# A hybrid decoder step on one core: the constants' place in VectorE's queue, and the PSUM banks of the output units

## The chip, the cores and the metric

The kernel runs on one core of one Trainium2 chip. The metric is the device time of one execution in microseconds (us), as the median of several runs. The engines are named as in the profile: PE is TensorE's matmuls and PEld its weight loads, DVE is VectorE, ACT is ScalarE, POOL is GpSimd, SP is SyncE, which here issues the DMAs (SPq).

## What is computed

The reference is one step of a decoder with two layers, for a prompt of 2048 tokens and a batch of 8 × 4 sample tokens, at a width of 1024. Cut to what matters:

```
def even_mixer(h, w_in, ...):                       # layer 0
    proj = h @ w_in
    qa, fa, ia, ga, qb, kb, vb, gb, fb = _split(proj, ...)
    f = lb + (1.0 - lb) * sigmoid(fa)
    o_a, s_a = gated_linear_chunked(qa, 1.0 - f, ia, log(f), hgrn_s0)
    o_a = head_rmsnorm(o_a, hgrn_gain) * silu(ga)
    o_b = fox_attend(qb, kb, vb, log_sigmoid(fb + b_fox)) * silu(gb)
    out = concatenate([o_a, o_b]) @ w_out
...
def odd_mixer(h, w_in, w_gate, ...):                # layer 1
    q, k, v, g, r = _split(h @ w_in, ...)
    log_f = log_sigmoid(r @ w_gate + b_gate) / 16
    o, s = gated_linear_chunked(q * scale, k, v, log_f, gla_s0)
    o = head_rmsnorm(o, gla_gain) * silu(g)
    return o @ w_out, s
...
x = x + even_mixer(rmsnorm(x, norm_even), ...)      # run_trunk
x = x + odd_mixer(rmsnorm(x, norm_odd), ...)
return rmsnorm(x, final_norm), ...                  # and the caches and states
```

`lb` is a softmax over the two rows of `lb_logits`; `fox_attend` is causal attention with forget gates, and for the sample tokens over paged caches.

## The kernel before, in words

Each large product is cut into **units**: 256 columns of a weight matrix by one half of the tokens (1024 prompt tokens, and in the half 0 the 32 sample rows as well). The operands are kept in two parts of 16 bits, so each product of a 128-row block is three matmuls (`mm3`, L595 to L597), and eight such blocks make a sum. A unit has four steps: `fetch` loads its raw weights (`wr_...`, L330), `measure` and `scale` find a power of two that fits them (VectorE's `rm_...` and `pow_...`, L264 to L305), and `split` makes the two parts (`w_...`: ScalarE L348, L354, L355, VectorE L349, POOL L356). They are run some units ahead (`staged`). `proj_fm` computes a unit with features on the partitions, in column pieces (`pf_...`); `proj_tm` computes one with tokens on the partitions, in pairs of 128-token tiles (`pt_...`), and `few_rows` adds the sample rows (`pS_...`).

The phase of layer 0 begins with the norm of the first half, in groups: ScalarE squares a row block (L429), VectorE makes the scale (L406, POOL L408) and scales the rows (`nx_...`, L431), TensorE transposes them (`nt_...`, L455), and ScalarE and VectorE in turn write the result in two parts (`act`, L590 and L591). The first unit, v0 (`pt_Av`), is multiplied beside these groups. The second unit, g0 (`pf_Ag`), makes the gate: `silu2` copies a piece (ScalarE L651), takes the tanh (`th_A`, L652) and multiplies it in (`sg`, VectorE L653). The third, qf0 (`pf_A00f`, weights `w_Aqf`), is the first to need `fa`, `fb` and `fbn`.

These, and other constants that no unit needs before, are made by `more_consts`: the gains `g_hgrn` and `g_gla` (L168), the chain of `lb` (L175 to L189, with two exponentials on ScalarE, L178 and L179), the gate's weights `wg` (a memset of `wgr` L194, three loads L196, ScalarE's copy L198, VectorE L199), seven masks `mlev` (POOL L206 to L210 into `mtmp`, a cast on VectorE L213), `mdiag` (L216) and zeros in two tiles `scT` (L235).

The order of each engine's queue is not the order of the code: the framework has a scheduler that runs a timeline of its own and puts every instruction where its operands allow it. `tc.issue_after(x)` holds it back: within it, the instructions of the engine that x runs on are put behind x; those of other engines aren't held. `more_consts` is called under three such holds: behind `last_x` (a load on SP), `last_a` and `last_th` (both on ScalarE). So VectorE's and POOL's constants are held by nothing but their operands.

Behind layer 0's attention stage the output projections run, four **out units** for each half and layer (`out_units`). In the trace the half 1 of layer 0 runs from about 1380 to 1481 us, and it is followed by the first units of layer 1 (`pt_Cv`, ...). While an out unit's tiles (`pt_o`) are multiplied, VectorE adds each to a block of x that has been loaded (`xo`, L1825), and the result is stored (L1827); beside it, the rows of x are normed for layer 1 (`x1r`, L533 to L547) and stored as `xs`, and DMA transposes bring them back as `act` (L565, on SP). An out unit has its own weights (`w_o`), prepared as above. `done` marks the last stage, in which the final norm is run beside it.

PSUM has eight banks, in four groups by tag: `pj` 3, `gr` 2, `st` 1 and `o` 2. All units' tiles come from `pj`; `gr` and `o` are those of the norm's transposes at the start, and later of the linear attention.

Of the kernel before, what the change touches and what calls it, by code (L numbers as in the profile page):

```python
# [8 lines left out]
F32 = mybir.dt.float32  # L9
# [6 lines left out]
ALU = mybir.AluOpType  # L16
# [3 lines left out]
P = 128  # L20
# [89 lines left out]
def drain(g):  # L110
    for _ in g:
        pass
# [11 lines left out]
class Kern:  # L124
    def __init__(self, ctx, tc, ins, outs):
        self.ctx, self.tc, self.nc = ctx, tc, tc.nc
        self.i, self.o = ins, outs
        self.loaded = {}


    def consts(self):
# [473 lines left out]
            evac(ps[:M, :n], c0, n)  # L605
            yield 24 * (n / 2.4 + 3)

    def proj_tm(self, pps, act, W, hf, evac, nm, width=256, pairs=True):

        tl = self.ttiles(hf)  # L610
        per = 2 if width == 256 and pairs else 1
        for g in range(0, len(tl), per):
            grp = tl[g : g + per]
            n = grp[0][1]
            if n < P:
                evac(self.few_rows(pps, act, W, grp[0][0], nm, width), g, 1, n)
                yield 700
                continue
            ps = pps.tile([P, per, width], F32, tag="pj", name=f"pt_{nm}{g}")
            for j, (c0, n) in enumerate(grp):  # L620
                for k in range(KT):
                    self.mm3(ps[:n, j], [x[:, k, c0 : c0 + n] for x in act],
                             [x[:, k, :width] for x in W], k == 0, k == KT - 1)
            evac(ps[:n, : len(grp)], g, len(grp), n)
            yield 24 * len(grp) * 110
# [21 lines left out]
    def silu2(self, wp, dst, ps, n, nm, c):  # L647

        nc = self.nc
        th = wp.tile([P, 512], F32, tag="th", name=f"th_{nm}")  # L650
        nc.scalar.activation(dst, ps, AF.Copy, scale=c)  # L651
        self.last_th = nc.scalar.activation(th[:, :n], dst, AF.Tanh, scale=0.5)  # L652
        nc.vector.scalar_tensor_tensor(dst, th[:, :n], 1.0, dst, ALU.add, ALU.mult)  # L653


    def lin_attn(self, wp, pps, hf, h, dv, q, f, k, v, vs, sg, gain, S, s0, s_out, p_out, ydst, nm):
# [418 lines left out]
    def phase_even(self):  # L1075
        tc, nc, i = self.tc, self.nc, self.i
# [3 lines left out]
        with pool("act", side="right") as ap, pool("w", side="right") as w0, pool("wl", side="right") as wp1, \  # L1080
# [4 lines left out]
            pps = Pool(pp0, {"pj": 3, "gr": 2, "st": 1, "o": 2})  # L1085
# [6 lines left out]
            act = self.alloc_act(ap)  # L1092
# [19 lines left out]
            for hf in range(2):  # L1112
# [7 lines left out]
                def dense(a, b, hf=hf):  # L1120
                    return self.staged(us, 16 * hf + a, 16 * hf + b, beside)

                lin = lins[hf]
                if hf == 0:
                    groups = self.norm_groups(nrm, pps, act, hf, get_x, self.g_even)
                    groups[0][0]()
                    for step in us[0][0]:
                        self.ready[0] = step()

                    for g in groups[1:3]:  # L1130
                        g[2]()

                    def behind(ins, g):
                        with tc.issue_after(ins.ins):
                            groups[g][0]()

                    def turn0():
                        groups[0][1](1, lambda st: st.enter_context(tc.issue_after(self.last_scale.ins)))

                    def turn1():  # L1140
                        groups[1][1](KT // 2 - 1, lambda st: behind(self.last_a, 2))
                        behind(self.last_a, 3)

                    steps = [lambda: None, lambda: behind(self.last_split, 1), lambda: None, lambda: None, groups[4][0]]
                    turns = [turn0, turn1] + [g[1] for g in groups[2:]]
                    first = self.handover(list(zip(steps, turns)), dense(0, 1), last)
                    drain(first)
                    second = dense(1, 2)
                    for _ in range(2):
                        next(second)  # L1150
                    with tc.issue_after(self.last_x.ins), tc.issue_after(self.last_a.ins), \
                            tc.issue_after(self.last_th.ins):
                        self.more_consts(wp)
                    drain(second)
                else:
                    self.sx_odd = self.gain_scale(self.g_odd, pps, "pj", "o")
                    self.later = [self.later_unit(wpool, pps, w, cols, key, undo) for w, cols, key, undo in
                                  self.later_units()]
                    first = dense(0, 1)
                    for g in nxt:  # L1160
                        c = next(last, None)
                        g[1]()
                    drain(last)
                    drain(first)
# [640 lines left out]
    def out_units(self, hf, layer, act, wpool, wp, pps, x2=None, done=None):  # L1805

        nc, i = self.nc, self.i
        w = i[("w_out_even", "w_out_odd")[layer]][0]

        def mk(u):  # L1810
            cs = slice(u * 256, (u + 1) * 256)
            undo = [self.kcol()] + ([self.kcol()] if layer == 0 and hf == 0 else [])

            def ev(ps, g, cnt, m):
                c0 = self.ttiles(hf)[g][0]
                c = undo[-1 if m < P else 0][:m]
                if x2 is None:
                    if layer:
                        t = wp.tile([P, 2, 256], F32, tag="c2", name=f"xo{layer}{hf}{u}{g}")
                    else:  # L1820
                        t = wp.tile([P, HALF + TS], F32, tag="c4", name=f"xo{layer}{hf}{u}{g}")[:, :512].rearrange(
                            "p (g d) -> p g d", g=2)
                    src = self.rows(hf, c0, m * cnt, layer == 0)[:, cs].rearrange("(g p) d -> p g d", g=cnt)
                    nc.sync.dma_start(t[:m, :cnt], src)
                    nc.vector.scalar_tensor_tensor(t[:m, :cnt], ps, c, t[:m, :cnt], ALU.mult, ALU.add)  # L1825
                    dst = self.rows(hf, c0, m * cnt, False)[:, cs].rearrange("(g p) d -> p g d", g=cnt)
                    nc.sync.dma_start(dst, t[:m, :cnt])  # L1827
                else:
                    for j in range(cnt):
                        d = x2[g + j][:m, cs]  # L1830
                        nc.vector.scalar_tensor_tensor(d, ps[:, j], c, d, ALU.mult, ALU.add)
                        if done:
                            done(u, g + j, x2[g + j], cs)
                        if layer == 0 and u == 3:
                            nc.sync.dma_start(self.rows(hf, c0 + j * P, m, False), x2[g + j][:m])

            return (self.half_unit(wpool, pps, w, [(u * 256, 256)], f"o{layer}{u}", f"o{layer}{hf}{u}",
                                   also=list(zip(undo, (self.sy[layer], self.sy[2]))),
                                   raw=("yr", 256) if (hf, layer, u) == (0, 0, 0) else ("wr", WU),
                                   scaler="pool" if (hf, layer, u) == (0, 0, 0) else None),  # L1840
                    lambda W: self.proj_tm(pps, act, W, hf, ev, f"o{layer}{hf}{u}", pairs=not done or u < 3))

        return [mk(u) for u in range(4)]


# [343 lines left out]
```

## Time and profile before

| | before |
|---|---|
| runs | 2366.59, 2371.02, 2367.46 us, median 2367.46 |
| profiled execution | 2365.9 us, its span 2364.2 |
| PE busy | 2265.2 us, 96% of the span |
| DVE, ACT, POOL busy | 59%, 46%, 35% |
| granted TensorE clock, mean | 0.989 |

The span goes from the first to the last instruction of the profiled execution; its own time includes what lies around it. Rows of the waits view give the engine, its tile and line, then whom it waited for: us in total, how often, the longest. Rows of the timeline give the start and the duration in us, the engine, the line, the operation and its tiles, and in brackets how long the engine had been idle before and what ended it. Rows of the windows view give a stretch, its length, busy us and count of instructions for PE, PEld, DVE, ACT and POOL, then the granted clock (1.00 is full), the DMA engines' share, and GB/s.

### The profile page before, as it was taken

The page shows a single profiled execution, that of the slowest core. Times are in us where ns is not written, and L with a number is a line of the kernel's source. Part 1 is how long each engine was busy: PE and PEld are TensorE (multiplying, and loading weights), DVE is VectorE, ACT ScalarE, POOL GpSimd, SP SyncE. Part 2 cuts the span into 40 slices and gives each one's busy share as a digit, 9 for nine tenths or more (in the row PEclk, how much of TensorE's full clock was granted, in tenths as well). Part 3 has the DMA queues.
Part 4 walks back from the last instruction along what each step waited for, and adds up shares of the span by engine and source line. Part 5 has one row for each costly group of instructions (what it writes and reads, how often), then busy time and mean ns, then how long its engine had stood idle before and what let it go on. Part 6 is the DMA issues. An engine that isn't in the chain of part 4 may idle for free. (4 is left out here: it accounts for less than half of the span.)

```text
span 2364.2 us, 58202 instructions
## 1 busy us (share of the span) xinstructions
PE 2265.2 (96%) x23124; PEld 1613.1 (68%) x23124; DVE 1404.4 (59%) x3225; ACT 1090.3 (46%) x2372; POOL 818.6 (35%) x858
## 2 busy tenths in 40 slices
PE   6999999999999999999999999999899999999998
PEld 5667667864655875655445888777677666666887
DVE  6656557536664538666767444366675655557554
ACT  5434343333333226556667543436545545545333
POOL 3133324112212226234557345144452422222223
PEclk9999999999999999999999999999999999999999
DMA  6231334755441267776873867633234431115453
GB/s 191 73 89 59 100 109 146 196 157 148 145 123 56 75 196 239 239 256 198 280 239 117 278 197 249 148 96 108 79 117 101 107 103 57 48 55 166 152 194 149
DMA packets 358004, 344.89 MB, mean 146 GB/s; under 512 B 90994, under 2 KB 300723, under 8 KB 357731
## 3 DMA queue, kind: packets, MB, share of 16 engines
q1 hardware_dynamic: 356226, 336.64, 46.8%
q8 instruction: 182, 2.98, 0.5%
q0 software_dynamic: 1504, 4.52, 0.5%
q14 instruction: 92, 0.75, 0.1%
HBM read 248.73 MB, written 79.63 MB: 139 GB/s over the span
## 5 line engine op out<-in xcount | busy, mean ns | idle before, releaser
L595 PE MATMUL pt_o<-w_o,act 128*128 128x256 f16 x1024 | 281.1, 274 | 8.2 <-DVE xo L1825 6.6
L597 PE MATMUL pt_o<-w_o,act 128*128 128x256 f16 x1024 | 281.0, 274 | 3.8 <-DVE act L1784 3.7
L596 PE MATMUL pt_o<-w_o,act 128*128 128x256 f16 x1024 | 281.1, 275 | 1.5 <-POOL w_o L356 1.5
L597 PEld LDWEIGHTS <-act 128*128 128x128 f16 x2304 | 227.3, 99 | 39.4 <-DVE act L1784 5.1
L596 PEld LDWEIGHTS <-act 128*128 128x128 f16 x2304 | 227.3, 99 | 38.5 <-issue 8.4
L595 PEld LDWEIGHTS <-act 128*128 128x128 f16 x2304 | 227.4, 99 | 35.9 <-issue 3.4
L761 POOL TENSOR_TENSOR kA<-kA,fA 128x512 f32<-128x512 f32 (+1 forms) x56 | 79.5, 1419 | 190.1 <-PE gl_A L727 141.9
L595 PE MATMUL pt_Cv<-w_Cv,act 128*128 128x256 f16 (+1 forms) x512 | 141.4, 276 | 0.0
L597 PE MATMUL pt_Cv<-w_Cv,act 128*128 128x256 f16 (+1 forms) x512 | 141.3, 276 | 0.0
L596 PE MATMUL pt_Cv<-w_Cv,act 128*128 128x256 f16 (+1 forms) x512 | 141.3, 276 | 0.0
L761 POOL TENSOR_TENSOR kC<-kC,fC 128x512 f32<-128x512 f32 (+1 forms) x56 | 83.6, 1493 | 153.8 <-PE gl_C L727 102.5
L1392 ACT ACTIVATE L<-L,nm,kc 128x512 f32<-128x512 f32 (+3 forms) x160 | 118.2, 741 | 33.5 <-DVE nm L1390 27.8
L1400 POOL TENSOR_SCALAR L<-L,nm 128x512 f32<-128x512 f32 (+3 forms) x160 | 99.0, 632 | 64.5 <-DVE nm L1396 23.9
L1427 ACT ACTIVATE th<-pt 128x512 f16<-128x512 f32 (+3 forms) x159 | 80.5, 528 | 64.5 <-PE pt L1420 63.6
L1428 DVE TENSOR_TENSOR tl<-pt,th 128x512 f16<-128x512 f32 (+3 forms) x159 | 94.6, 609 | 21.4 <-ACT th L1427 20.5
L1420 PE MATMUL pt<-ident,L 128*128 128x128 f32 x544 | 91.2, 279 | 7.1 <-POOL L L1400 4.2
L1420 PEld LDWEIGHTS pt<-ident,L 128*128 128x128 f32 x544 | 66.6, 143 | 33.3 <-DVE tl L1428 8.3
L1544 PEld LDWEIGHTS pkt<-ident,pgcache_fox_k 128*128 128x128 f32 x512 | 57.4, 141 | 42.7 <-issue 25.1
L1877 ACT ACTIVATE vC<-pt_Cv,kc 128x512 f32<-128x512 f32 (+1 forms) x40 | 23.9, 598 | 129.9 <-PE pt_Cv L597 129.9
L1544 PE MATMUL pkt<-ident,pgcache_fox_k 128*128 128x128 f32 x512 | 75.1, 278 | 7.3 <-DVE kts L1548 5.1
L1825 DVE SCALAR_TENSOR_TENSOR xo<-pt_o,kc,xo 128x512 f32<-128x512 f32 x48 | 35.8, 748 | 62.0 <-PE pt_o L597 57.2
L597 PE MATMUL pt_Av<-w_Ai,act 128*128 128x256 f16 x256 | 70.9, 277 | 1.5 <-DVE act L591 1.5
(957 smaller groups left out, 6788.5 us busy)
## 6 DMA issues: line engine op xcount, KB each, us to landing
pgcache_fox_k<-in_cache_fox_k SPq DMA_DIRECT2D x128, 256.0 KB, 4.4
pgcache_fox_v<-in_cache_fox_v SPq DMA_DIRECT2D x128, 256.0 KB, 4.3
yr<-yT SPq DMA_DIRECT2D x16, 1024.0 KB, 7.2
x1d<-xo SPq DMA_DIRECT2D x48, 256.0 KB, 4.1
wr_Aqf<-in_w_in_even SPq DMA_DIRECT2D x64, 128.0 KB, 3.2
wr_o<-in_w_out_even SPq DMA_DIRECT2D x32, 256.0 KB, 6.0
xo<-in_x_prompt SPq DMA_DIRECT2D x32, 256.0 KB, 4.2
wr_Cv<-in_w_in_odd SPq DMA_DIRECT2D x32, 256.0 KB, 3.8
```

The source lines that it names most:

```text
L595: nc.tensor.matmul(ps, lh[0], rh[0], start=first, stop=False)
L596: nc.tensor.matmul(ps, lh[0], rh[1], start=False, stop=False)
L597: return nc.tensor.matmul(ps, lh[1], rh[0], start=False, stop=last)
L761: nc.gpsimd.tensor_tensor(kv[:, :, 0], kv[:, :, 0], t1.to_broadcast([P, nb, w]), ALU.mult)
L1392: self.last_exp = nc.scalar.activation(lt[:, :w], lt[:, :w], AF.Exp, bias=nm[:, 0:1], scale=ib, accum_out=nm[:, 2 + j : 3 + j])
L1400: nc.gpsimd.tensor_scalar(lt[:, :w], lt[:, :w], nm[:, 1:2], 2.0**14, ALU.mult, ALU.mult)
L1420: nc.tensor.transpose(pt[:, w : w + P], rows[b][s // 4][0][:, (s % 4) * P : (s % 4 + 1) * P], self.ident)
L1427: nc.scalar.activation(th[:, a:w], pt[:, a:w], AF.Copy),
L1428: nc.vector.tensor_tensor(tl[:, a:w], pt[:, a:w], th[:, a:w], ALU.subtract)))
L1544: nc.tensor.transpose(pk[:, j * P : (j + 1) * P], pgs[j][:, h * P : (h + 1) * P], self.ident)
L1825: nc.vector.scalar_tensor_tensor(t[:m, :cnt], ps, c, t[:m, :cnt], ALU.mult, ALU.add)
L1877: r = nc.scalar.activation(v[h][:, g : g + cnt], ps[:, :, :256], AF.Copy, scale=c)
```

## The change

Two things are changed. In `phase_even`, the third hold of `more_consts` is on `last_si`, the multiplication with which `silu2` ends (VectorE), in place of `last_th`, the tanh (ScalarE); at that point of the code the last of them is that of g0's second column piece. And `proj_tm` takes a list of tags, through which a counter turns from tile to tile: for the out units of the half 0 and half 1 of layer 0 and for half 1 of layer 1 it has seven entries in all, as many as the banks of `pj`, `gr` and `o` together; elsewhere it is `pj` as before. The sample rows' tile (`few_rows`) remains on `pj`.

```
-        self.loaded = {}
+        self.loaded, self.bank = {}, 0
...
-    def proj_tm(self, pps, act, W, hf, evac, nm, width=256, pairs=True):
+    def proj_tm(self, pps, act, W, hf, evac, nm, width=256, pairs=True, banks=("pj",)):
...
-            ps = pps.tile([P, per, width], F32, tag="pj", name=f"pt_{nm}{g}")
+            ps = pps.tile([P, per, width], F32, tag=banks[self.bank % len(banks)], name=f"pt_{nm}{g}")
+            self.bank += 1
...
-        nc.vector.scalar_tensor_tensor(dst, th[:, :n], 1.0, dst, ALU.add, ALU.mult)
+        self.last_si = nc.vector.scalar_tensor_tensor(dst, th[:, :n], 1.0, dst, ALU.add, ALU.mult)
...
                     with tc.issue_after(self.last_x.ins), tc.issue_after(self.last_a.ins), \
-                            tc.issue_after(self.last_th.ins):
+                            tc.issue_after(self.last_si.ins):
                         self.more_consts(wp)
...
-            cs = slice(u * 256, (u + 1) * 256)
+            cs, free = slice(u * 256, (u + 1) * 256), (hf, layer) != (0, 1)
...
-                    lambda W: self.proj_tm(pps, act, W, hf, ev, f"o{layer}{hf}{u}", pairs=not done or u < 3))
+                    lambda W: self.proj_tm(pps, act, W, hf, ev, f"o{layer}{hf}{u}", pairs=not done or u < 3,
+                                           banks=("pj", "gr", "pj", "o", "pj", "gr", "o") if free else ("pj",)))
```

What follows is the order in which the built programs' instructions stand. On VectorE before, from the second group of row blocks on, constants stand among the norm's steps (`rst_n`, `nx`, and the splits into `act`):

```order
L406 TENSOR_SCALAR rst_n_250<-nss_248 128x1
L213 CAST mlev_841<-mtmp 128x64
L168 TENSOR_SCALAR g_hgrn<-g_hgrn 128x4
L168 TENSOR_SCALAR g_gla<-g_gla 128x8
L591 SCALAR_TENSOR_TENSOR act<-nt_4_263,g_even,act 128x256
L264 TENSOR_REDUCE kc<-g_odd 128x1
L264 TENSOR_REDUCE kc<-g_hgrn 128x1
L264 TENSOR_REDUCE kc<-g_gla 128x1
L431 TENSOR_SCALAR nx_512_167<-nx_512_167,rsr_n_252 128x1024
L591 SCALAR_TENSOR_TENSOR act<-nt_5_268,g_even,act 128x256
```

The same place on VectorE after the change:

```order
L406 TENSOR_SCALAR rst_n_250<-nss_248 128x1
L431 TENSOR_SCALAR nx_512_167<-nx_512_167,rsr_n_252 128x1024
L591 SCALAR_TENSOR_TENSOR act<-nt_4_263,g_even,act 128x256
L264 TENSOR_REDUCE kc<-g_odd 128x1
L591 SCALAR_TENSOR_TENSOR act<-nt_5_268,g_even,act 128x256
L406 TENSOR_SCALAR rst_n_258<-nss_256 128x1
L591 SCALAR_TENSOR_TENSOR act<-nt_6_273,g_even,act 128x256
```

The cast and the gains have left, and so have, a few rows on, the sums of `lb` (L175 to L177); only the column of `g_odd` remains. They now stand here on VectorE, behind the step of g0's second piece (`th_A_758`) and ahead of the scale of the third unit's weights (`pow_Aqf`, L274):

```order
L654 SCALAR_TENSOR_TENSOR sg_697<-th_A_758,sg_697 128x352
L168 TENSOR_SCALAR g_hgrn<-g_hgrn 128x4
L168 TENSOR_SCALAR g_gla<-g_gla 128x8
L175 TENSOR_TENSOR lb<-lb 128x4
L194 MEMSET wgr 80x512
L216 CAST mdiag<-ident 128x128
L235 MEMSET scT_863 128x1024
L235 MEMSET scT_864 128x1024
L297 TENSOR_REDUCE rm_Bq_1069<-rm_Bq_1069 128x1
L274 TENSOR_SCALAR kc<-pow_Aqf_764 128x1
L213 CAST mlev_811<-mtmp 128x64
```

Before, only a step of `lb` (L180), `wg` (L199) and the row `rm_Bq` stood between that step and the scale, and the memsets were the first of VectorE's work. On ScalarE at the same place of the program, before the change:

```order
L178 ACTIVATE lb<-lb 128x4
L179 ACTIVATE lb<-lb 128x4
L198 ACTIVATE wg<-wgr 80x512
L651 ACTIVATE sg_697<-pf_Ag_876,kc 128x352
L652 ACTIVATE th_A_901<-sg_697 128x352
L354 ACTIVATE wr_Aqf_561<-wr_Aqf_561,kc 128x2x256
```

and after it:

```order
L652 ACTIVATE sg_697<-pf_Ag_876,kc 128x352
L653 ACTIVATE th_A_901<-sg_697 128x352
L198 ACTIVATE wg<-wgr 80x512
L178 ACTIVATE lb<-lb 128x4
L179 ACTIVATE lb<-lb 128x4
L652 ACTIVATE sg_916<-pf_Ag_917,kc 128x352
L354 ACTIVATE wr_Aqf_561<-wr_Aqf_561,kc 128x2x256
```

The copy of `wg` and the exponentials moved behind g0's third piece, and a fourth piece (`pf_Ag_917`) moved ahead of the third unit's weights. On POOL the masks (L206 to L210) now stand between the weights of g0 and those of the third unit (L356), and on SP the loads of `wgr`, which follow its memset, stand behind those of `wr_Bq`. In the stages of the out units every engine's order is the same before and after; there only the banks differ.

## Prediction

> **What bounds the kernel.** I read the page first: the span, the busy times of the engines, and the forty slices of TensorE.
>
> ```profile
> span 2364.2 us, 58202 instructions
> PE 2265.2 (96%) x23124; PEld 1613.1 (68%) x23124; DVE 1404.4 (59%) x3225; ACT 1090.3 (46%) x2372; POOL 818.6 (35%) x858
> ...
> PE   6999999999999999999999999999899999999998
> ```
>
> TensorE is busy for 2265.2 of 2364.2 us, so the bound is TensorE, and no edit that leaves its matmuls alone can win more than the 99 us in which it idles. The first slice (59 us) is the only one at 6; all others read 9, but for two at 8. The change works on the first slice and, with the banks, on the output units, so I asked for TensorE's waits in those two places. First, the waits from 20 to 50 us (columns: us in total, times, longest).
>
> ```profile
> PE nt L455 <- DVE act L591: 4.6, 2, 4.0
> PE pt_Av L597 <- DVE act L591: 1.5, 1, 1.5
> PE pt_Av L595 <- ACT act L590: 0.9, 1, 0.9
> PE nt L455 <- DVE nx L431: 0.4, 1, 0.4
> ```
>
> These sum to 7.4 us, and one wait of 4.0 is more than half. VectorE's timeline and SyncE's queue show what stands behind it.
>
> ```profile
> 22.27 0.20 DVE L213 CAST mlev<-mtmp 128x64 int8<-128x64 f32 x1 [0.86 <-POOL mtmp L210]
> ...
> 28.37 0.17 DVE L168 TENSOR_SCALAR g_hgrn<-g_hgrn 128x4 f32<-128x4 f32 x1 [1.13 <-DMA g_hgrn<-in_hgrn_gain]
> ...
> 35.10 0.16 DVE L175 TENSOR_TENSOR lb<-lb 128x4 f32<-128x4 f32 x1 [2.99 <-DMA lb<-in_lb_logits]
> ...
> 38.93 2.24 DVE L591 SCALAR_TENSOR_TENSOR act<-nt,g_even,act 128x256 f16<-128x256 f32 x5
> ```
>
> ```profile
> 27.59 4.97 SPq L330 DMA_DIRECT2D wr_Aqf<-in_w_in_even  x8
> 32.61 0.47 SPq L174 DMA_DIRECT2D lb<-in_lb_logits  x1
> ```
>
> ```profile
> 39.45 0.69 PE L455 MATMUL nt<-ident,nx 128*128 128x128 f32 x2 [4.00 <-DVE act L591]
> ```
>
> The second load of lb (2 KB) stands on SyncE's queue behind eight weight loads of 4.97 us. VectorE, in order, waits 2.99 us for it at 35.10, and everything behind it is late: the scaling of the last norm groups and the splits at 38.93 that free TensorE's transposes at 39.45. None of the constants in this queue is needed by the first unit.
>
> The waits of the output units 4 to 7 (1380 to 1481 us) are one line:
>
> ```profile
> PE pt_o L595 <- DVE xo L1825: 6.6, 5, 2.0
> ```
>
> A tile of the output projection waits until VectorE has read an older tile out of its bank. VectorE is held by work for the next unit's input, two row scalings of over 6 us while POOL runs the same kind:
>
> ```profile
> 1409.88 6.23 DVE L547 SCALAR_TENSOR_TENSOR x1r<-x1r,rsr_n 32x1024 f16<-32x1024 f32 x2 [0.35 <-ACT x1r L546]
> ```
>
> **The change, part by part.** Sums are made against the profiled execution: 2365.9 us, 1.7 us over its span, and 1.56 us under the median of the runs (2367.46). A difference is added to the median.
>
> *Waits at the start.* The constants of VectorE now stand behind the second column piece of g0, half a hundred us from here, as the order shows. The wait of 4.00 us goes in full: 2.99 of it is the wait for lb itself, the rest the casts (about 0.2 us each, and waits like the 0.86) and the 1.13 for g_hgrn that pushed VectorE back earlier. Of the other 3.4 us I take a quarter, 0.9, because part of it waits for ScalarE's half of the same splits, and SyncE's order and ScalarE's squares stay. That is **−4.9**, between −2.99 (only the wait for lb) and −7.4 (all four lines).
>
> *The clock at 39.3.* The windows view names the granted clock and the matmuls per stretch.
>
> ```profile
> 39.30:42.70 3.40, 3.25 (x15) 2.70 (x16) 2.24 (x6) 1.33 (x3) 0.00 (x0) 0.50 0.99 310
> 42.70:46.10 3.40, 3.40 (x34) 3.15 (x32) 2.94 (x6) 2.46 (x6) 0.00 (x0) 1.00 0.08 24
> ...
> 1431.90:1435.30 3.40, 3.40 (x19) 2.42 (x17) 0.92 (x2) 0.00 (x0) 3.40 (x2) 0.50 0.85 233
> ```
>
> After the wait of 4.00 us TensorE works 3.4 us at clock 0.50: half of 3.25 busy us, 1.6 us, is lost. With the wait gone I take **−1.4**, between −1.6 and 0 (a remainder of the waits may still bring the window on). The Trainium skill's "TensorE: Matmul & The Clock Gate", section "HAM oscillation — how this bites in real kernels", asks for no idle gap over about 3.4 us: by that rule the clock falls at 39.3, where the trace agrees (4.00 idle, then 0.50), but it would not fall at 1431.9, where the longest wait of the stage is 2.0 us and the trace shows 0.50 all the same. The measurement decides, and a clock term therefore belongs to the second part too.
>
> *The banks.* The output units of both halves, save those run beside the last attention, now spread over seven banks instead of three. A tile then may wait four tiles longer for VectorE, so the 6.6 us go, and with them the half clock at 1431.9 (half of 3.40, 1.7 us): 8.3 us. TensorE cannot keep it all. Unit 8 (pt_Cv) reads rows that DMA transposes bring:
>
> ```profile
> act<-xs SPq DMA_TRANSPOSE x17, 5.3
> ```
>
> ```profile
> 1493.99 2.17 SPq L565 DMA_TRANSPOSE act<-xs  x1
> ```
>
> ```profile
> 1501.42 0.28 PE L595 MATMUL pt_Cv<-w_Cv,act 128*128 128x272 f16 x1
> ```
>
> The last transpose is issued at 1493.99 and lands, by the median of 5.3, about 1499.3; its tile starts at 1501.42. So 2.1 us of run-ahead are left there, at most 5.3 if it is counted from the end of its issue (1496.16). SyncE's order in this stage is unchanged and is paced by its own transfers, so TensorE arriving sooner does not move it. I take **−2.75**, near the median's end, between 0 and −8.3.
>
> *The third unit's weights.* The constants do not vanish: they now stand ahead of the scale of Aqf0, the third unit, on three engines. Before:
>
> ```profile
> 68.60 0.55 ACT L651 ACTIVATE sg<-pf_Ag,kc 128x352 f32<-128x352 f32 x1 [2.01 <-PE pf_Ag L597]
> ...
> 69.59 0.71 ACT L354 ACTIVATE wr_Aqf<-wr_Aqf,kc 128x512 f32<-128x512 f32 x1
> ```
>
> ```profile
> 72.73 2.31 POOL L356 TENSOR_TENSOR w_Aqf<-wr_Aqf,w_Aqf 128x512 f16<-128x512 f32 x2 [15.70 <-ACT w_Aqf L355]
> ```
>
> ```profile
> 79.21 0.31 PE L597 MATMUL pf_Ag<-act,w_Ag 128*128 128x352 f16 x1
> 79.36 0.31 PE L595 MATMUL pf_A00f<-act,w_Aqf 128*128 128x352 f16 x1
> ```
>
> The weights were ready at 72.73 + 2.31 = 75.04 and first used at 79.36: a cover of 4.3 us. Now ScalarE copies the next piece of g0 (pf_Ag_917) ahead of the weights; a piece is 24 matmuls at 0.15, so it ends 3.6 after the one at 68.60, and the weights start at 72.2 + 0.55 = 72.75 instead of 69.59, 3.2 later. VectorE agrees: the scale of Aqf0, which ScalarE's 69.59 waits for, now follows two memsets of scT, that of wgr, and some short ones,
>
> ```profile
> 1.12 0.91 DVE L235 MEMSET scT<- 128x1024 f32 x1 [0.19 <-issue]
> ```
>
> ```profile
> 18.03 0.48 DVE L194 MEMSET wgr<- 80x512 f32 x1
> ```
>
> 2 × 0.91 + 0.48 = 2.3 us, and with the short ones (each like the 0.16 at 35.10) about as late as ScalarE's 3.2. On SyncE the loads of wgr wait for that memset, which follows g0's second piece; that piece's last step on VectorE lies a little before 68.60, the memset ends about 69.1, so they are issued to 70.5
>
> ```profile
> 33.73 1.38 SPq L196 DMA_DIRECT2D wgr<-in_w_gla_gate  x3
> ```
>
> and land by their median
>
> ```profile
> wgr<-in_w_gla_gate SPq DMA_DIRECT2D x3, 32.0 KB, 1.8
> g_hgrn<-in_hgrn_gain SPq DMA_DIRECT2D x1, 2.0 KB, 5.9
> ```
>
> near 71.9; the copy L198 (0.6), two exponentials (0.3) and the piece (0.55) stand between it and the weights, 73.3. So 0.5 us of the cover is left and POOL's chain of masks (three short instructions for each of seven levels) lies in POOL's wait of 15.70. I take **+0.4**: the cover holds at the median (0), and a landing like g_hgrn's 5.9 would cost 4.1 − 0.5 = 3.6, plus 1.7 of clock: +5.3.
>
> *The fox stage.* TensorE comes there earlier, and its first stretches are short of data:
>
> ```profile
> 872.00:879.00 7.00, 4.05 (x27) 2.08 (x24) 3.93 (x19) 2.64 (x8) 3.21 (x6) 1.00 1.04 344
> ```
>
> The DMA engines are full (1.04), TensorE works 4.05 of 7 us. Part of what the start won waits here. Pages are asked for by ring slots that earlier steps free, so they come sooner too; I take **+1.0**, between 0 and +6.3 (all of the start, 4.9 + 1.4).
>
> Sum: −4.9 − 1.4 − 2.75 + 0.4 + 1.0 = −7.65. The profiled time would be 2358.2, the median **2359.8 us**.
>
> **The rivals.**
> - *The fox stage takes the start back.* For it: the DMA share of 1.04. Against: TensorE's slices there (879 to 1380 us) read 9, so over most of the stage it is TensorE that sets the pace, and a page that was asked for sooner lands sooner. −7.65 + 5.3 = −2.35: 2365.1.
> - *The banks bring nothing*, since the stage's end is set by the transposes alone. Then −4.9: 2362.6. Against: at least 2.1 us are free at the last one.
> - *The transposes come sooner with TensorE*, as the stores they follow are released by VectorE's reads. Then −8.3 stands for −2.75: −13.2, 2354.3. Against: SyncE issues them among loads and stores whose own landings pace it.
> - *The third unit waits for late constants.* Place: ScalarE's L198, which holds back the piece and the weights. Price: 1 us for each us that wgr lands later than 2.3 us after its last issue, and 1.7 for the clock. It makes the kernel slower than before from 2.3 + 7.65 + 0.4 − 1.7 = 8.65 us on; at 10 us, 2368.8. For it: g_hgrn's 5.9. Against: 1.8 in the row of wgr itself, and the queues are quiet near 45 (share 0.08).
> - *A long wait at unit 8 halves the clock.* What TensorE wins and cannot keep, 8.3 − 2.75 = 5.55 us, becomes a wait ahead of a pt_Cv tile, above the 4.00 that brought 0.50 at 39.3. That costs 1.7 after it, in tiles with nothing else to wait for: 2361.5. This is what the skill's rule above would do here.
> - *More banks, lower clock.* Each bank change idles TensorE a little, and the clock falls. A fall costs 1.7 us, and some 50 tiles use the seven banks: up to 85 us, so some 2400 at a third of them. Against: tiles change among three banks now, and the clock stands at 1.00 while no wait comes between:
>
> ```profile
> 1380.00:1394.00 14.00, 14.00 (x145) 12.09 (x143) 4.06 (x5) 8.35 (x15) 5.53 (x5) 1.00 0.86 275
> ```
>
> The skill's same page warns of this in "A second HAM failure mode: psum-queue depth-cycling"; no run here shows it.
>
> **How the numbers follow.** The forecast has 0.54, the fox stage 0.16, no gain from the banks 0.11, sooner transposes 0.07, the late constants 0.05, the clock at unit 8 0.05, and lower clock by banks 0.02. 0.2%, about what a measurement of this kernel can tell from no change, is 4.7 us: the bound is 2362.7. Of the forecast about a tenth spills over it (0.05), and half of the rival at 2362.6. Faster: 0.49 + 0.05 + 0.07 + 0.05 = 0.66. The same: 0.05 + 0.06 + 0.16 = 0.27. Slower: 0.07. The range runs from the sooner transposes, 2354.0, to a little over the fox rival, 2366.5, and leaves the slower cases out.
>
> **What would show it.** The waits at 20 to 50 us should shrink to about 2.5 us with no 4.0, and the clock at 35 to 46 stay at 1.0. VectorE should run its lb, casts and memsets behind g0's second piece, and pf_A00f should start without a wait for w_Aqf. The line pt_o <- xo should go from the stage 1375 to 1475, and a wait of pt_Cv for the transposes (act <- xs) should come in its place. The prediction is wrong if the third unit waits over 2 us, if the fox stage starts no earlier than before, or if the last transpose is issued at other than about its old distance from the stage's start.

## The result, and the profile after

| | before | after |
|---|---|---|
| median | 2368.57 us (8 runs, 2361.15 to 2373.07) | 2359.31 us (8 runs, 2357.72 to 2365.06) |
| ratio to before | | 0.9965, 95% interval 0.9954 to 0.9977 |
| profiled execution | 2365.9, span 2364.2 | 2362.66, span 2361.0 |

The change gains 9.3 us of the medians, by the interval between 5 and 11. The two profiled executions differ by 3.2 us only: the one of before is 2.7 us under its median, the one of after 3.4 us over its own. So single executions are read here by their parts, and the totals by the medians.

The page after, its head and TensorE's slices:

```profile
span 2361.0 us, 58204 instructions
PE 2267.8 (96%) x23124; PEld 1614.2 (68%) x23124; DVE 1404.2 (59%) x3225; ACT 1090.5 (46%) x2372; POOL 816.5 (35%) x858
...
PE   7999999999999999999999999999899999999998
```

The first slice has risen from 6 to 7. (Line numbers behind an edit shift by the lines that it adds: L1825 before is L1826 after.) TensorE's waits from 20 to 50 us after the change:

```profile
PE pS_Av L640 <- DVE sam_Av L635: 1.0, 1, 1.0
PE nt L455 <- DVE act L591: 0.6, 1, 0.6
PE pt_Av L595 <- ACT act L590: 0.5, 1, 0.5
PE nt L455 <- DVE rst_n L406: 0.5, 1, 0.5
```

7.4 us have become 2.6, and the wait of 4.0 is gone. VectorE's constants stand where the order put them, the first step of lb (L175) with no wait:

```profile
61.42 0.52 DVE L654 SCALAR_TENSOR_TENSOR sg<-th_A,sg 128x352 f32<-128x352 f32 x1
61.85 0.17 DVE L168 TENSOR_SCALAR g_hgrn<-g_hgrn 128x4 f32<-128x4 f32 x1
61.93 0.17 DVE L168 TENSOR_SCALAR g_gla<-g_gla 128x8 f32<-128x8 f32 x1
62.00 0.16 DVE L175 TENSOR_TENSOR lb<-lb 128x4 f32<-128x4 f32 x1
```

The third unit begins at 73.12, where it began at 79.36 before, 6.24 us sooner, and no wait stands before it:

```profile
73.12 0.31 PE L595 MATMUL pf_A00f<-act,w_Aqf 128*128 128x352 f16 x1
```

In the stage from 1370 to 1500 the waits pt_o <- xo (6.6 us) are gone, and one line has come in their place:

```profile
PE pt_Cv L595 <- DMA act<-xs: 3.6, 4, 2.5
```

```profile
1468.17 0.29 PE L595 MATMUL pt_Cv<-w_Cv,act 128*128 128x272 f16 x1 [2.46 <-DMA act<-xs]
```

Unit 8 began at 1481.52 before; it is 13.35 us sooner now. The start's 6.24 had become 7.13 by the first out unit (1292.16 for 1299.29), so the banks let TensorE run ahead by 6.2 us more here, and by 8.7 before the wait of 2.46. What becomes of it is seen by following the difference, landmark by landmark (us against before, from the timelines of TensorE; unit 11 is the second `pt_Cv`):

| | before (us) | after |
|---|---|---|
| first pf_A00f | 79.36 | −6.24 |
| first pt_o | 1299.29 | −7.13 |
| first pt_Cv (unit 8) | 1481.52 | −13.35 |
| first pf_C00q (unit 9) | 1505.56 | −9.55 |
| first zC | 1516.67 | −8.43 |
| first pt_Cv of unit 11 | 1551.62 | −6.62 |
| span | 2364.2 | −3.2 |

By unit 11 the whole gain of the banks has been taken back: −6.62 is the −7.13 with which the stage began. One part goes to the transposes, as forecast. The other goes in unit 9, 2.9 us from its first matmul to unit 11: 1.83 in a wait of a z tile (`zC`) at 1514.12, most of the rest in two short waits before it (0.55 and 0.34). This row of the waits from 1490 to 1610 us (after, and before under it) holds that wait and a second one of 1.05 at 1590, which lies behind unit 11:

```profile
PE zC L1919 <- ACT qC L1933: 2.9, 2, 1.8
```

```profile
PE zC L1917 <- ACT qC L1931: 0.2, 1, 0.2
```

ScalarE and SyncE after the change say why:

```profile
1512.90 0.72 ACT L354 ACTIVATE wr_Cv<-wr_Cv,kc 128x512 f32<-128x512 f32 x1 [2.57 <-DMA wr_Cv<-in_w_in_odd]
1513.53 0.54 ACT L1933 ACTIVATE qC<-pf_C00q,kc 128x352 f32<-128x352 f32 x1
```

```profile
1487.23 2.10 SPq L565 DMA_TRANSPOSE act<-xs  x1
...
1493.19 3.47 SPq L330 DMA_DIRECT2D wr_Cg<-in_w_in_odd  x4
...
1506.77 1.91 SPq L330 DMA_DIRECT2D wr_Cv<-in_w_in_odd  x4
```

The copy qC, for which TensorE waits, stands on ScalarE behind the scaling of the next raw weights (`wr_Cv`), and these weights were asked for at 1506.77. That issue did not follow the transposes at once. SyncE waited ahead of it for VectorE's split of the weights before (`w_Cv`), as long as in the kernel before:

```profile
SPq L330 <- DVE w_Cv L349: 10.1, 1, 10.1
```

That split follows ScalarE's part of it, and ScalarE had waited for the raw weights of `Cg`, which SyncE issued behind the last transpose:

```profile
1500.37 0.72 ACT L354 ACTIVATE wr_Cg<-wr_Cg,kc 128x512 f32<-128x512 f32 x1 [2.49 <-DMA wr_Cg<-in_w_in_odd]
```

So the way from the transposes to the wait at 1514.12 leads twice through SyncE's queue. Before, the issue of `wr_Cv` stands at 1513.64 (6.87 later), the last transpose at 1493.99 (6.76 later). In this execution, SyncE's queue has moved by what the start gave and by nothing more.

From unit 11 to the end this execution loses another 3.4 us: the second of these waits, and stretches at half clock near 1592 and 2172 us that before's execution lacks, 1.7 us each at most. Where such stretches fall differs among the executions that were traced, and whether the change has a part in these two stays open.

### The profile page after: what moved, and what is told of

Same layout as the page of the kernel before. It is cut to its first block, busy times and chain, and to the rows that moved or that the text cites. A ratio compares the mean times of both kernels' runs of the same rounds, so it can differ in the third digit from the quotient of the medians.

```text
span 2361.0 us, 58204 instructions
## 1 busy us (share of the span) xinstructions
PE 2267.8 (96%) x23124; PEld 1614.2 (68%) x23124; DVE 1404.2 (59%) x3225; ACT 1090.5 (46%) x2372; POOL 816.5 (35%) x858
## 5 line engine op out<-in xcount | busy, mean ns | idle before, releaser
L597 PE MATMUL pt_o<-w_o,act 128*128 128x256 f16 x1024 | 281.1, 274 | 4.0 <-DVE act L1785 3.6
L596 PE MATMUL pt_o<-w_o,act 128*128 128x256 f16 x1024 | 281.1, 275 | 1.5 <-POOL w_o L356 1.5
L597 PEld LDWEIGHTS <-act 128*128 128x128 f16 x2304 | 227.4, 99 | 38.0 <-DVE act L1785 5.0
L596 PEld LDWEIGHTS <-act 128*128 128x128 f16 x2304 | 227.4, 99 | 31.5 <-issue 1.5
L596 PE MATMUL pt_Cv<-w_Cv,act 128*128 128x256 f16 (+1 forms) x512 | 142.1, 278 | 0.0
L597 PE MATMUL pt_Cv<-w_Cv,act 128*128 128x256 f16 (+1 forms) x512 | 142.0, 277 | 0.0
L1429 DVE TENSOR_TENSOR tl<-pt,th 128x512 f16<-128x512 f32 (+3 forms) x159 | 94.5, 608 | 21.9 <-ACT th L1428 20.9
L595 PE MATMUL pt_Av<-w_Ai,act 128*128 128x256 f16 x256 | 71.1, 278 | 0.5 <-ACT act L590 0.5
L596 PE MATMUL pt_Av<-w_Ai,act 128*128 128x256 f16 x256 | 70.9, 277 | 0.4 <-DVE w_Ai L349 0.4
```

The lines of the kernel that those rows point to most:

```text
L595: nc.tensor.matmul(ps, lh[0], rh[0], start=first, stop=False)
L596: nc.tensor.matmul(ps, lh[0], rh[1], start=False, stop=False)
L597: return nc.tensor.matmul(ps, lh[1], rh[0], start=False, stop=last)
L1429: nc.vector.tensor_tensor(tl[:, a:w], pt[:, a:w], th[:, a:w], ALU.subtract)))
```

## The experiments

Theory A: the start is nearly all of the gain, since what the banks win is given back to a queue of transfers that a ring of buffers paces (a load of a block of x waits until the store of the block that had its buffer before has landed). Theory B: the banks keep 2.75 us, as predicted.

**The constants' part alone.**

```
-                                           banks=("pj", "gr", "pj", "o", "pj", "gr", "o") if free else ("pj",)))
+                                           banks=("pj",)))
```

> Only the constants' part of the change; the output units keep their three banks. Theory A (the start is nearly all of the gain, and what the banks win is taken back by the queue of transfers behind the output units): TensorE's lag against before is about -6.2 us from 50 us on and about the same at the end but for half-clock windows, so the time is 5.5 to 7.5 us under before, within 1.5 us of the full change. Theory B (the banks keep 2.75 us, as the prediction has it): 2 to 3.5 us slower than the full change. In both, the waits pt_o <- xo of 6 to 7 us in the second half's output units of layer 0 are back.

Measured: 2357.47 us (6 runs) beside 2365.84 of before, a ratio of 0.9954 (0.9941 to 0.9967; the ratios on record are not plain quotients of the medians, which give 0.9965 here). That is no worse than the full change (0.9965, 0.9954 to 0.9977). The third unit begins at 72.38, 6.98 us sooner than before, and the waits are back:

```profile
PE pt_o L595 <- DVE xo L1826: 6.8, 5, 2.0
```

B, by which this run is 2 to 3.5 us slower than the full change (0.9974 to 0.9980), lies outside the interval of this run. This speaks against B without excluding it: the full change's 0.9965 has an interval as wide, and by the quotients of the medians (0.9965 and 0.9961) this run is 0.9 us the slower one. A's "the same at the end" held by the medians, which lie 8.4 us under before in place of the 5.5 to 7.5; the profiled execution (2363.35, the slowest of the six) lost 4.2 us between the third unit and the first pt_o and ends 2.5 us under before.

**The banks' part alone.**

```
-                            tc.issue_after(self.last_si.ins):
+                            tc.issue_after(self.last_th.ins):
```

> Only the banks' part of the change; the constants stand as before. Theory A: the waits pt_o <- xo go, TensorE reaches unit 8 about 9 us sooner, and has given it all back 40 us later, by waits for the transposes, and then by z tiles that wait for ScalarE, which waits for the next raw weights; the time is within 1.5 us of before. Theory B: the time is 2 to 3.5 us under before.

Measured: 2364.89 us (12 runs) beside 2365.84, a ratio of 0.9996 (0.9981 to 1.0010): no gain that can be told from none. B's 2 to 3.5 us (0.9985 to 0.9992) lie inside this interval, so it is the trace that speaks for A. Its waits from 1370 to 1500 are

```profile
PE pt_Cv L595 <- DMA act<-xs: 4.1, 4, 1.7
```

and its course is the one that A gave: −0.6 us at the first pt_o, −8.9 at unit 8, −4.4 at the first zC, −1.2 at unit 11. Eight us of run-ahead are won, and all but 0.6 of them are given back in 80 us.

**One load for lb**, in the kernel before:

```
-            for r, t in enumerate((l0, l1)):
-                nc.sync.dma_start(t, i["lb_logits"][r].rearrange("(k p) -> p k", p=P))
+            nc.sync.dma_start(lb[:, : 2 * NH].rearrange("p (r k) -> p r k", r=2),
+                              i["lb_logits"].rearrange("r (k p) -> p r k", p=P))
```

> The kernel before, with the two rows of lb loaded by one transfer in place of two, so that nothing of lb stands behind the weight loads on SyncE's queue. If the wait for lb alone (2.99 us on VectorE, 4.00 on TensorE) is what the start loses, VectorE's wait ahead of L175 goes and TensorE's lag after 50 us is -3 to -4 us, the casts and gains costing the other 2 to 3. If the casts and gains among the norm's steps are the larger part, the lag is under 2 us.

Measured: a ratio of 0.9980 (0.9966 to 0.9994). The third unit begins at 76.19, so 3.17 us sooner than before. The row that waited 2.99 us is worth 3.2 us of TensorE; the casts and gains, and the other waits, are worth the other 3.1 of the 6.24. These are single executions: in two others with the constants as before (banks alone, and buffers alone below), the third unit begins at 78.13 and 79.35, so about 1 us of each difference can be scatter. The bounds of the first term were drawn from the right rows.

**Nine buffers for the blocks of x**, on top of the change:

```
-        self.loaded, self.bank = {}, 0
+        self.loaded, self.bank, self.slot = {}, 0, 0
...
-                        t = wp.tile([P, HALF + TS], F32, tag="c4", name=f"xo{layer}{hf}{u}{g}")[:, :512].rearrange(
+                        self.slot += 1
+                        t = wp.tile([P, HALF + TS], F32, tag=("c4", "c4", "sg")[self.slot % 3],
+                                    name=f"xo{layer}{hf}{u}{g}")[:, :512].rearrange(
```

> The changed kernel, with the blocks of x of layer 0's output units in nine buffers (c4 and sg in turn) in place of six of c4. Theory A says that SyncE's queue is paced by a ring: a load waits until a store of six blocks ago has landed, and each such wait holds back all that stands behind it on the queue, the transposes for unit 8 and then the next raw weights too. With nine buffers the loads' waits for the stores (33.6 us in all between 1375 and 1500) go to under 10, the last transpose is issued 5 to 9 us sooner against the stage's start, and 4 to 9 us more are kept: 2350 to 2356. A rival says that the transposes are paced by their own transfers or by TensorE's reads of the old act: then the queue's waits change their name, and the time stays within 2 us of the full change.

Measured: 2350.55 us (5 runs, 2349.58 to 2352.7) beside 2365.84, a ratio of 0.9930 (0.9916 to 0.9943). This version beats both kernels. Its last transposes and next weights on SyncE:

```profile
1477.50 2.41 SPq L565 DMA_TRANSPOSE act<-xs  x1
...
1498.37 1.91 SPq L330 DMA_DIRECT2D wr_Cv<-in_w_in_odd  x4
```

9.7 and 8.4 us sooner than in the changed kernel. From 1370 to 1500 TensorE waits for nobody, and the windows view gives for the stretch that was the output units' stage before

```profile
1380.00:1481.00 101.00, 101.00 (x936) 89.53 (x935) 48.09 (x70) 41.69 (x66) 50.61 (x32) 1.00 0.88 246
```

101 us busy of 101, at full clock; unit 8 begins within it, at 1466.84. From the first pt_o to unit 11 the difference against before grows from −6.46 to −15.75, where the change alone went from −7.13 to −6.62: 9.3 us are kept. Two numbers of A's were missed. Counted from the first pt_o, the last transpose is issued 10.4 us sooner than in the changed kernel, not 5 to 9. And the loads' waits for the stores were to fall from 33.6 us to under 10; they fell to 21.9 (after the change, then with nine buffers):

```profile
SPq L1825 <- DMA x1d<-xo: 33.6, 12, 5.8
```

```profile
SPq L1827 <- DMA x1d<-xo: 21.9, 10, 4.3
```

The ring still turns tight, but it is no longer what ends last.

**The nine buffers without the banks** were tried twice, with the constants' part and on the kernel before.

> The constants' part and the nine buffers for x, with three banks as before. If late loads of x were what held VectorE's adds, and so the three banks, then the waits pt_o <- xo shrink from 6.8 us to under 3 and the time is within 1.5 us of the run with seven banks and nine buffers, about 2351 to 2353: then the banks are worth nothing by themselves even when the queue lets them. If VectorE's row scalings (6.2 us for two) are what holds them, the waits stay at 5 to 7 us, and the run is 4 to 8 us slower than with the seven banks, 2355 to 2358.

> The kernel before with the nine buffers for x and nothing else. If the buffers let the queue run sooner but three banks still make TensorE wait, the time is within 2 us of before; if the loads alone were what TensorE waited for, it is 5 to 9 us under before.

With the constants' part: 2358.33 us (9 runs) beside 2367.30, 0.9962 (0.9950 to 0.9974); against 0.9930 for banks and buffers, this is 7.6 us more. The waits are

```profile
PE pt_o L595 <- DVE xo L1828: 5.5, 4, 2.8
```

so VectorE still makes three banks wait, though the last transpose is issued at 1480.89 (13.1 us sooner than before): late loads aren't what holds the adds (VectorE's waits in this stage name no load ahead of them). On the kernel before: 0.9990 (0.9977 to 1.0004), within noise; its profiled execution has the waits at 8.6 us. So in this stage two limits stand in a row. Either edit alone gives nothing that the medians can tell (0.9996 and 0.9990; and 0.9962 against the constants' 0.9954). Both together give 6 to 8 us (0.9930 against 0.9954 and 0.9965).

**Unit 9 in every execution.** The step at which the change lost its last 1.8 us can be read in all traces. Against before, in us: the first `zC`, the issue of the raw weights `wr_Cv`, how much further TensorE has moved than that issue, and the wait of the z tile behind the copy qC.

| | first zC | issue of wr_Cv | TensorE further by | wait |
|---|---|---|---|---|
| the change | −8.43 | −6.87 | 1.56 | 1.83 |
| the change, later third unit (below) | −9.13 | −7.58 | 1.55 | 1.78 |
| banks alone | −4.41 | −2.85 | 1.56 | 1.59 |
| constants alone | −2.90 | −1.48 | 1.42 | 1.44 |
| one load for lb | −4.70 | −3.94 | 0.76 | 0.72 |
| the change and nine buffers | −14.68 | −15.27 | −0.59 | none |
| constants and nine buffers | −6.12 | −6.71 | −0.59 | none |
| nine buffers alone | +8.36 | +7.77 | −0.59 | none |

In the kernel before, the tile starts 0.05 us behind the end of the copy (1520.15 + 0.54):

```profile
1520.15 0.54 ACT L1931 ACTIVATE qC<-pf_C00q,kc 128x352 f32<-128x352 f32 x1
```

```profile
1520.74 0.42 PE L1917 MATMUL zC<-rT,wg 80*128 80x352 f32 x1
```

There was no slack here to begin with, so whatever TensorE gains on that issue it loses at once, with three banks as with seven. In the run with the constants alone, TensorE comes to the first zC 2.9 us sooner than before and reaches unit 11 0.2 us later: the wait of 1.44 takes a part of it, and a stretch at half clock behind it (0.50 from 1522.1 to 1523.8) takes more. Whether the banks by themselves move the issue a little can't be read from single executions: from the first pt_o on it moves against before by +0.3, −3.9 and −2.2 us with seven banks (the first three rows), and by +1.3 and −2.9 with three (the next two).

**A later third unit**: the changed kernel with the two memsets of scT made twice.

```
-        for t in self.scT:
+        for t in self.scT * 2:
             nc.vector.memset(t, 0.0)
```

> The changed kernel, with the two memsets of scT made twice, the second pair standing on VectorE between the copy of the third unit's exponent and the rest of its scale: 2.1 us more ahead of these weights. If the cover at the third unit is used up by the change, TensorE waits 1.5 to 2.1 us at pf_A00f for w_Aqf, and its lag is smaller by that from 75 us on. If half a microsecond of cover is left, as the prediction has it, the wait is 1.0 to 1.6 us; if the cover is still more than 2 us, there is no wait.

Measured, one execution: the third unit begins at 73.19, and no wait is listed. The weights now come at the last moment:

```profile
72.67 1.15 POOL L356 TENSOR_TENSOR w_Aqf<-wr_Aqf,w_Aqf 128x512 f16<-128x512 f32 x1
```

```profile
73.64 0.31 PE L596 MATMUL pf_A00f<-act,w_Aqf 128*128 128x352 f16 x1
73.87 0.32 PE L597 MATMUL pf_A00f<-act,w_Aqf 128*128 128x352 f16 x1
```

The step from L596 to L597 is 0.23 in place of 0.15: TensorE waited 0.08 us for the piece that ended at 73.82. None of the three expectations fits: there is no wait to speak of, though the cover was not over 2 us. In the changed kernel POOL reached the same piece at 71.09,

```profile
71.09 2.26 POOL L356 TENSOR_TENSOR w_Aqf<-wr_Aqf,w_Aqf 128x512 f16<-128x512 f32 x2
```

1.58 us sooner, so the cover that the change left was about 1.5 us: more than the 0.5 of the prediction, less than 2.

## Why the prediction was right, point by point

The forecast was −7.65 us; the medians gave −9.3 (5 to 11 by the interval), and the landmarks −6.6 at unit 11. The mechanism of the start was right and carries nearly all of the gain; that of the banks was wrong. That the sum came out is in part luck: the −2.75 for the banks was not there, and the +1.4 for the third unit and the fox stage, which the landmarks don't show either, made up for half of it. And the medians of the change, of the constants alone and of the constants with nine buffers lie 9.3, 8.4 and 9.0 us under before, 1 to 3 us more than the traces show at the third unit (6.2 to 7.2); where these lie stays open.

- **The start: −6.3 forecast (−4.9 and −1.4), −6.24 measured.** The waits gave 4.8 of 7.4 (7.4 to 2.6), near the −4.9. The clock term did not come as forecast in this execution: the half clock moved from 39.3 to 29.0. Three of the experiments' executions have nearly the same waits and no such window, and they begin the third unit 7.0 to 7.2 us sooner. So such a window costs 0.7 to 0.9 us here, and the change does away with it in some executions only.
- **The third unit: +0.4 forecast, 0 measured.** ScalarE's scaling of the weights began where the sum had it (at 66.66, which is 3.3 us later against TensorE than before, where it had 3.2 to 3.7). What ended last was not ScalarE but POOL: its masks waited for VectorE's casts, and ran from 65.15 to 71.1, right ahead of the weights, where the prediction had them in POOL's idle time. Yet nothing was lost: TensorE needs only the first of POOL's two pieces, and now at its fifth matmul (73.72), where the prediction's cover counted both pieces against the first matmul.

```profile
66.66 0.71 ACT L354 ACTIVATE wr_Aqf<-wr_Aqf,kc 128x512 f32<-128x512 f32 x1
```

```profile
65.15 0.15 POOL L206 MEMSET mtmp<- 128x64 f32 x1 [12.90 <-DVE kc L264]
```

- **The fox stage: +1.0 forecast, neither shown nor refuted.** In the changed kernel the difference was −6.24 at the third unit and −7.13 at the first pt_o, so nothing was lost. But from one execution to the next this way varies by more than the term: with the constants' part 0.7, 0.8, 2.5 and 4.2 us are lost in the other runs, with one load for lb 2.1, and where the start is as before 0.6 and 4.7.
- **The banks: −2.75 forecast, about 0 measured (0.9996 alone, which leaves some 3 us either way).** This step failed. Its first half held: the waits went, unit 8 waited for the transposes, and −9.55 at the start of unit 9 against −7.13 at the first pt_o leaves 2.4 us, near the 2.1 to 2.75 of the sum. But the sum stopped there. The same queue that carried the late transposes carried the next raw weights behind them, and ScalarE's order put TensorE's copy behind these: 2.9 more us went in unit 9, where the kernel before had no slack. "TensorE arriving sooner does not move it" was true of all that stands behind on that queue, and the forecast should have asked at each later need, not at the first.
- **The rivals.** "The banks bring nothing", with a chance of 0.11 and 2362.6 us, was what happened to the banks, though by another mechanism: at least 2 us were free at the last transpose, as the prediction said, and were lost at the next transfer. "Sooner transposes" did not happen in this execution; with nine buffers they came. "A long wait at unit 8 halves the clock" did happen, at a wait of 2.46 in place of 5.55: the stretch after it stands at 0.52.

```profile
1465.80:1469.20 3.40, 1.03 (x9) 0.89 (x10) 0.70 (x1) 0.00 (x0) 0.00 (x0) 1.00 0.95 209
1469.20:1472.60 3.40, 3.40 (x18) 2.31 (x17) 0.00 (x0) 0.00 (x0) 0.00 (x0) 0.52 1.14 255
```

Beside the waits for the transposes, which hold back the next tiles too, it cost nothing that shows: with the banks alone the clock stays at 1.00 from 1465 to 1500, and from unit 8 to unit 9 TensorE loses 3.8 us there as here (−8.93 to −5.12, and −13.35 to −9.55). "More banks, lower clock" is refuted by the run with nine buffers: its 101 us at 1.00 cycle through the seven banks up to 1466.84; what the Trainium skill's page "TensorE: Matmul & The Clock Gate" warns of in "A second HAM failure mode: psum-queue depth-cycling" does not occur here.

## What to carry to other kernels

A wait removed in the middle of a program is worth only what the next shared queue lets through. Follow the run-ahead to every later point at which the faster engine needs something from that queue, also through other engines' orders, until the queue has slack again. Where two edits each measure nothing, look whether they stand in series: here seven banks alone and nine buffers alone gave nothing that the medians could tell, and together 6 to 8 us. And constants that no early unit needs cost the most where they wait for a small transfer behind large ones: one load in place of two gave about half of what moving all of them gave.

## What the runs showed of the hardware

The clock fell without any long wait. From 25.6 to 29.0 us the longest wait of TensorE in the changed kernel is 0.57 us, but it is busy for 1.84 us of 3.40 only; the next stretch stands at 0.51:

```profile
25.60:29.00 3.40, 1.84 (x14) 0.94 (x12) 2.11 (x7) 3.40 (x9) 0.74 (x2) 0.98 1.07 66
29.00:32.40 3.40, 3.40 (x18) 2.63 (x17) 2.34 (x7) 3.37 (x9) 1.02 (x3) 0.51 0.73 173
```

So the length of the longest wait does not decide. The busy share of the stretch just before (54% here) doesn't either. Ahead of the half clock at 1431.9 before, TensorE was busy for 1.44 of 3.40 us (42%, the longest wait 2.0). Two stretches earlier it was busy for little more, 1.56 (46%), and kept its clock:

```profile
1421.70:1425.10 3.40, 1.56 (x15) 1.24 (x14) 1.04 (x4) 1.47 (x5) 2.93 (x3) 1.00 1.03 342
1425.10:1428.50 3.40, 3.40 (x34) 3.04 (x32) 2.26 (x2) 3.40 (x6) 3.40 (x2) 1.00 0.99 277
```

In the changed kernel the clock fell behind a stretch with 2.04 of 3.40 (60%), whose longest wait is 1.05 us:

```profile
1588.80:1592.20 3.40, 2.04 (x10) 1.17 (x9) 1.00 (x5) 3.21 (x7) 0.74 (x1) 1.00 0.05 12
1592.20:1595.60 3.40, 3.40 (x15) 2.31 (x15) 2.56 (x6) 3.38 (x8) 0.00 (x0) 0.50 0.03 5
```

What tells the stretches that lower the clock from those that don't stays open.
